# Moving GpSimd's work in a kernel's input stage to VectorE, and one reduction ahead of three tiles

## The chip, the cores and the metric

One core of a Trainium2 chip runs the whole program in one launch. The engines of a core work at the same time, each through a queue of its own in order: TensorE (PE in the profile; its weight loads are PEld), VectorE (DVE), ScalarE (ACT), GpSimd (POOL) and SyncE (SP), which here issues nearly all DMAs. They wait for each other through semaphores. The metric is the device time of one execution in microseconds (us), less is better.

## What is computed

Two layers over 1024 tokens of width 1024, in float32. The first is latent attention: an input projection gives 384 q latents, 256 kv latents, 64 shared rotary key columns and 1024 gate columns; the latents are normalised and projected to 8 heads. The second is a gated convolution module (31 taps). Cut to the part that the change touches:

```python
h = rmsnorm(x, mla_norm_g)
z = h @ w_in                                   # 1024 x 1728
q_lat, kv_lat, k_pe, gate = split(z, [384, 640, 704])
q  = rmsnorm(q_lat, q_norm_g) @ w_qb           # 8 heads of 128 + 64 rotary
kv = rmsnorm(kv_lat, kv_norm_g) @ w_kvb
q_pe, k_pe = apply_rope(q_pe), apply_rope(k_pe)
x = x + (attention(q, k, v) * silu(gate)) @ w_out
# then the convolution layer, x + ..., and a last rmsnorm
```

## The kernel before, in words

Activations lie transposed, 128 channels by 1024 tokens to a tile. Each matrix product is made of three passes over rounded numbers: every operand is split into a high half (rounded) and a low half (what the rounding left), and a product is high x high, high x low, low x high (`mm3`, lines 136 to 139: L137, L138 and L139 in the profile). So each weight tile that arrives needs a copy on ScalarE (`wh_...`, L104) and a subtraction (`wl_...`, L106), and the third matmul of a tile is the first that reads the low half. In `load_w` the subtraction is GpSimd's unless the caller names an engine; in `split_early`, which splits weights of the second layer early and stores their low halves (`sl_cg`, L120) in DRAM for later, it is GpSimd's too.

The input stage, the first 196 us, runs so:

- Three accumulators (`acc3`: kv latents and rotary key) are built while x arrives, and VectorE adds up the squares of x (`ssum`).
- Then come eleven tiles `in_tile(n)`, named b0 to b10, of 48 matmuls each: b0 to b2 are the q latents, b3 to b10 the gates of the eight heads. Between b8 and b9 stand four tiles for the rotary part of q (`ps_qr`, 18 matmuls each).
- For the scale of a norm, squares are added up tile by tile (`lat_evac`, L302: `zskv`, `zsq_`), then `col_sums32` folds the 1024 sums of a row: a transposition on VectorE (L158), a reduction on VectorE (L160, `part...`), and one small matmul (L162, `cskv`, `csq`), after which small instructions give the scale, which goes out to DRAM and comes back spread over all partitions (`spread_dma`: `rowq`, then `Fq`). `lat_norm` does that for the kv latents after b1 and for the q latents after b5.
- VectorE also computes the angles of the rotary tables meanwhile (`trig_...`, about 25 instructions for each half of the tokens, L369 to L385), and multiplies each gate tile out of PSUM (`gt`, L340).

PSUM has six accumulator buffers in this stage, so a tile of matmuls needs the one of three tiles earlier to have been emptied. Weight tiles rotate through five buffers (`w`), raw weights through two (`wraw`).

TensorE's order is the program's (a manual schedule). The order of the other engines is worked out when the kernel is built, by a scheduler with a model of its own; it stands fixed in the program. After the input stage GpSimd scales the softmax rows, adds products in the convolution, and scales outputs at the end.

Of the kernel before, what the change touches and what calls it, by code (L numbers as in the profile page):

```python
# [18 lines left out]
P = 128  # L19
# [45 lines left out]
def hybrid_body(ctx, tc, xT, xP, pos, cols, w1a, w1b, wqr, wqk, wv, wo, wc, we, out):  # L65
# [15 lines left out]
    ones = const.tile([P, P], F32, name="ones")  # L81
    g.memset(ones, 1.0)

# [4 lines left out]
    warm = const.tile([P, 1], F32, name="warm")  # L88
    s.activation(warm, ones[:, 0:1], AF.Copy)
    small = ctx.enter_context(tc.tile_pool(name="small", bufs=1))  # L90
# [5 lines left out]

    def load_w(src, n, nm, alloc=None, eng=g):
        if alloc is None:
            def alloc(name):
                return wp.tile([P, 1024], F32R, tag="w", bufs=5, name=name)  # L100
        raw = wp.tile([P, 1024], F32, tag="wraw", name=f"wr_{nm}")
        sp.dma_start(raw[:, :n], src)
        hi = alloc(f"wh_{nm}")
        s.activation(hi[:, :n], raw[:, :n], AF.Copy)  # L104
        lo = alloc(f"wl_{nm}")
        eng.tensor_tensor(lo[:, :n], raw[:, :n], hi[:, :n].bitcast(F32), ALU.subtract)  # L106
        return hi, lo
# [4 lines left out]
    def split_early(src, nm):  # L112
        raw = wp.tile([P, 1024], F32, tag="wraw", name=f"sr_{nm}")
        sp.dma_start(raw, src)
        hi = wp.tile([P, 1024], F32R, tag="w", bufs=5, name=f"sh_{nm}")
        lo = wp.tile([P, 1024], F32R, tag="w", bufs=5, name=f"sl_{nm}")
        for a in range(2):
            cs = sl(a, CH)
            s.activation(hi[:, cs], raw[:, cs], AF.Copy)
            g.tensor_tensor(lo[:, cs], raw[:, cs], hi[:, cs].bitcast(F32), ALU.subtract)  # L120
        loS[nm] = tc.dram_tile([P, 1024], F32, name=f"loS{nm}")
        sp.dma_start(loS[nm], lo.bitcast(F32))
# [30 lines left out]

    def col_sums32(src, ntok, tile_, alloc, nm):

        n = ntok // 32
        tr = tile_.rearrange("p (j f) -> p j f", f=32)
        v.transpose(tr, src.rearrange("p (r j) -> p j r", r=32))  # L158
        part = small.tile([P, 32], F32, tag="part", bufs=1, name=f"part{nm}")[:, :n]
        reduced[nm] = v.tensor_reduce(part, tr, AX.X, ALU.add)  # L160
        ps = alloc(f"cs{nm}")[:, :n]
        pe.matmul(ps, mod32, part, start=True, stop=True)  # L162
        return ps
# [96 lines left out]
    for k in range(KD):  # L260
        xs[k] = ar.tile([P, T], F32, tag="zg", bufs=5, name=f"xs{k}")
        if k == 0 or k % 2 == 1:
            first, many = k, 1 if k in (0, KD - 1) else 2
            pair = load_w(w1a[:, 384 * k : 384 * (k + many)], 384 * many, f"a{k}", eng=v)
        wh, wl = (w_[:, 384 * (k - first) : 384 * (k - first + 1)] for w_ in pair)
        for c in range(2):
            sp.dma_start(xs[k][:, sl(c, CH)], xT[sl(k), sl(c, CH)])
        if k == 0:
# [13 lines left out]

    def lat_norm(zg, zs, n, gname, dh, dl, nm):
        F = tmp(f"F{nm}")
        Fc = inv_sqrt(col_sums32(zs, T, F, pstat, nm), 1.0 / (n * P), 1e-6, nm, extra=Rc)
        Fr = small.tile([P, 32], F32, tag="Fr", bufs=1, name=f"Fr{nm}")
        v.tensor_tensor(Fr, Fc, Rc, ALU.mult)
        spread_dma(Fr, T, F, nm)
        for i in range(n):
            v.scalar_tensor_tensor(zg[i], zg[i], cc(gname, i), F, ALU.mult, ALU.mult)  # L290
            s.activation(dh[i], zg[i], AF.Copy)
            v.tensor_tensor(dl[i], zg[i], dh[i].bitcast(F32), ALU.subtract)

    def lat_evac(ps, zg, zs, i, nm):
        for c in range(2):
            s.activation(zg[i][:, sl(c, CH)], ps[c], AF.Copy)
        if i == 0:
            s.activation(zs, zg[i], AF.Square)
        else:
            sq = tmp(f"zsq{nm}{i}")  # L300
            s.activation(sq, zg[i], AF.Square)
            g.tensor_tensor(zs, sq, zs, ALU.add)  # L302

    def in_tile(n):
        wh, wl = load_w(w1b[n], 1024, f"b{n}")
        ps = []
# [25 lines left out]
    ps_q1 = in_tile(1)  # L332
    lat_norm(zgkv, zskv, NKV, "gkv", kvh, kvl, "kv")
    ps_q2 = in_tile(2)
# [11 lines left out]
    for i, ps in enumerate((ps_q0, ps_q1, ps_q2)):  # L346
        lat_evac(ps, zgq, zsq_, i, "q")
    for h in range(3):
        gate_tile(h)
        split_early(wc[16 + h], f"cg{h}")  # L350
    lat_norm(zgq, zsq_, NQL, "gq", qnh, qnl, "q")


# [45 lines left out]
    def rope_pair(pr):  # L399
# [13 lines left out]
        for j in range(2):  # L413
            t1, t2 = tmp(f"rt1{pr}{j}"), tmp(f"rt2{pr}{j}")
            v.tensor_tensor(t1, A if j == 0 else B, cosT, ALU.mult)
            g.tensor_tensor(t2, B if j == 0 else A, sinT, ALU.mult)
            v.tensor_tensor(t1, t1, t2, ALU.subtract if j == 0 else ALU.add)
# [12 lines left out]
    gate_tile(7)  # L430

    es_pe.close()
    es_ap.close()
# [538 lines left out]
    def e_out(part):  # L972
# [9 lines left out]
        for m in range(KD):  # L982
# [6 lines left out]
            if c == 0:  # L989
                sp.dma_start(out[sl(m), cols_], x_)  # L990
            elif m % 2:
                sp.dma_start(out[sl(m // 2, 2 * P), cols_].rearrange("(a p) n -> p a n", a=2),
                             x1p[m // 2][:, :, n0:n1])
# [112 lines left out]
```

## Time and profile before

| | |
|---|---|
| three runs | 919.27, 922.48, 923.67 us (median 922.48) |
| the profiled execution | 922.44 us |
| its span, first to last instruction | 920.7 us |
| busy: PE, PEld, DVE, ACT, POOL | 897.9, 746.5, 648.8, 504.6, 440.6 us |
| mean granted clock of TensorE | 0.990 of full speed |
| input stage, to the last gate matmul | about 0 to 192 us of the span |

Of the page, part 1 gives the busy time of each engine; part 2 cuts the span into 40 slices and shows, under PEclk, the clock that TensorE was granted. The view of waits lists for each engine whom it waited for and how long. The view of windows gives busy times and the granted clock of chosen stretches. The timeline has one line for each instruction, or for several equal ones in a row (`x3`), with its start, its duration, and in brackets how long its engine had been idle and what ended that.

### The profile page before, as it was taken

Reading aid. Unit: us, or ns where it says so; the run is one execution under the profiler, and the core shown is the slowest. Engines: PE = TensorE matmul, PEld = TensorE weight load, DVE = VectorE, ACT = ScalarE, POOL = GpSimd, SP = SyncE. Lnnn points to the kernel's source line nnn. Section 1 sums busy time; section 2 is a strip of 40 time slices with the busy share of each in tenths; the row PEclk is TensorE's granted clock in tenths of the full one; section 3 lists DMA queues with packets and bytes.
Section 4 is the critical chain, followed back from the end, with each engine's and each line's share of the span. In section 5 each row is a group of like instructions: output and inputs, shape, how many; then the busy total and the mean of one; then the engine's idle time right before and its main releaser. Section 6 shows DMA issues by size and latency. Waiting matters only on the chain.

```text
span 920.7 us, 12418 instructions
## 1 busy us (share of the span) xinstructions
PE 897.9 (98%) x4432; PEld 746.5 (81%) x4432; DVE 648.8 (70%) x1073; ACT 504.6 (55%) x839; POOL 440.6 (48%) x370
## 2 busy tenths in 40 slices
PE   9999799999999999999999999999999999999996
PEld 7888588788898888978887887888888887778996
DVE  7478943756566656667454858999999998697543
ACT  8535244346465545565343446766666774677732
POOL 0333442725263332443234449999999993000034
PEclk9999989999999999999999999999999999999998
DMA  7214453485062232352183421111112322245714
GB/s 265 91 70 126 153 198 141 145 281 154 22 203 84 62 125 84 126 194 92 43 294 92 159 82 47 46 47 46 46 47 69 94 101 99 73 137 175 271 65 138
DMA packets 39662, 110.19 MB, mean 120 GB/s; under 512 B 5232, under 2 KB 8304, under 8 KB 39600
## 3 DMA queue, kind: packets, MB, share of 16 engines
q1 hardware_dynamic: 39520, 109.14, 35.6%
q8 instruction: 35, 0.57, 0.3%
q14 instruction: 27, 0.22, 0.1%
q0 software_dynamic: 80, 0.26, 0.1%
HBM read 83.93 MB, written 24.92 MB: 118 GB/s over the span
## 4 chain that ended last, share of the span: by engine, by line
PE 84%; DVE 7%; DMA 3%; ACT 2%; POOL 1%; issue 1%; SPq 0%; DVEq 0%; ACTq 0%; POOLq 0%
PE e L137 3%; PE e L139 3%; PE cb L138 3%; PE e L138 3%; PE cb L139 3%; PE cb L137 3%; PE cg L137 3%; PE cg L138 3%; PE cg L139 3%; PE T L545 3%; PE ca L137 3%; PE ca L139 3%; PE ca L138 3%; PE o L139 3%; PE o L137 3%; PE o L138 3%
## 5 line engine op out<-in xcount | busy, mean ns | idle before, releaser
L797 POOL TENSOR_TENSOR dcv<-dcv,pkb 128x512 f32<-128x512 f32 (+1 forms) x126 | 157.9, 1256 | 8.6 <-ACT pkb L796 1.0
L796 ACT ACTIVATE pkb<-u,taps 128x512 f32<-128x512 f32 (+1 forms) x126 | 83.8, 675 | 55.6 <-POOL dcv L797 50.8
L532 POOL TENSOR_SCALAR P<-P,st 128x128 f32<-128x128 f32 (+3 forms) x64 | 48.4, 757 | 122.5 <-DVE st L531 115.4
L808 DVE SCALAR_TENSOR_TENSOR av<-u,taps,av 128x512 f32<-128x512 f32 (+1 forms) x135 | 91.7, 687 | 1.2 <-ACT av L802 1.1
L810 DVE SCALAR_TENSOR_TENSOR cv<-su,gsum,cv 128x512 f32<-128x512 f32 (+1 forms) x117 | 80.6, 689 | 0.4
L987 POOL TENSOR_TENSOR x<-x,rbe 128x512 f32<-128x512 f32 (+1 forms) x16 | 16.2, 1051 | 127.0 <-DMA rbe<-rowe 127.0
L554 ACT ACTIVATE pth<-T 128x512 fp32r<-128x512 f32 (+1 forms) x96 | 46.1, 490 | 51.2 <-PE T L545 44.0
L555 DVE TENSOR_TENSOR ptl<-T,pth 128x512 fp32r<-128x512 f32 (+1 forms) x96 | 52.3, 554 | 30.4 <-ACT pth L554 30.0
L139 PE MATMUL ps_b<-xgh,wl_b 128*128 128x512 f32 x176 | 70.7, 402 | 1.2 <-POOL wl_b L106 1.2
L137 PE MATMUL ps_b<-xgh,wh_b 128*128 128x512 f32 x176 | 70.8, 403 | 0.0
L138 PE MATMUL ps_b<-xgl,wh_b 128*128 128x512 f32 x176 | 70.5, 401 | 0.0
L106 POOL TENSOR_TENSOR wl_o<-wr_o,wh_o 128x1024 fp32r<-128x1024 f32 x16 | 39.4, 2465 | 59.2 <-PE o L139 30.3
L137 PE MATMUL e<-a_y,wh_e 128*128 128x256 f32 (+1 forms) x192 | 61.7, 322 | 0.0
L139 PE MATMUL e<-a_y,wl_e 128*128 128x256 f32 (+1 forms) x192 | 61.5, 320 | 0.0
L138 PE MATMUL e<-a_y,wh_e 128*128 128x256 f32 (+1 forms) x192 | 61.4, 320 | 0.0
L529 ACT ACTIVATE P<-S,st 128x128 f32<-128x128 f32 (+3 forms) x64 | 47.5, 742 | 23.9 <-DVE st L527 18.7
L106 POOL TENSOR_TENSOR wl_b<-wr_b,wh_b 128x1024 fp32r<-128x1024 f32 x11 | 31.0, 2817 | 53.9 <-PE acc L138 36.7
L137 PE MATMUL cg<-a_h,wh_cg 128*128 128x512 f32 x128 | 51.7, 404 | 0.0
L138 PE MATMUL cb<-a_h,wh_cb 128*128 128x512 f32 x128 | 50.8, 397 | 0.8 <-DVE a_h L727 0.8
L139 PE MATMUL o<-a_og,wl_o 128*128 128x512 f32 x128 | 51.0, 398 | 0.3 <-POOL wl_o L106 0.3
L137 PE MATMUL o<-a_og,wh_o 128*128 128x512 f32 x128 | 51.0, 400 | 0.0
L137 PE MATMUL cb<-a_h,wh_cb 128*128 128x512 f32 x128 | 50.8, 397 | 0.0
(320 smaller groups left out, 2730.2 us busy)
## 6 DMA issues: line engine op xcount, KB each, us to landing
wr_o<-in_wo_dram SPq DMA_DIRECT2D x16, 512.0 KB, 4.1
wr_e<-in_we_dram SPq DMA_DIRECT2D x14, 512.0 KB, 4.6
wl_e<-loSe SPq DMA_DIRECT2D x14, 512.0 KB, 3.9
wr_b<-in_w1b_dram SPq DMA_DIRECT2D x11, 512.0 KB, 3.3
xs<-in_xT_dram SPq DMA_DIRECT2D x16, 256.0 KB, 5.6
sr_cg<-in_wc_dram SPq DMA_DIRECT2D x8, 512.0 KB, 4.5
loScg<-sl_cg SPq DMA_DIRECT2D x8, 512.0 KB, 3.8
gateS<-gt SPq DMA_DIRECT2D x8, 512.0 KB, 2.8
```

What stands on the lines that cost most here:

```text
L106: eng.tensor_tensor(lo[:, :n], raw[:, :n], hi[:, :n].bitcast(F32), ALU.subtract)
L137: pe.matmul(ps, wh, xh, start=start, stop=False)
L138: pe.matmul(ps, wh, xl, start=False, stop=False)
L139: pe.matmul(ps, wl, xh, start=False, stop=stop)
L529: s.activation(pr[:, :nk], ps[:, off : off + nk], AF.Exp, bias=st[:, 0:1], accum_out=st[:, 1:2])
L532: g.tensor_scalar(pr[:, :nk], pr[:, :nk], st[:, 2:3], 1.0, ALU.mult, ALU.mult)
L554: s.activation(hi[:, n0:], pt[:, n0:], AF.Copy)
L555: v.tensor_tensor(lo[:, n0:], pt[:, n0:], hi[:, n0:].bitcast(F32), ALU.subtract)
L796: s.activation(pk, lag(src, i), AF.Copy, scale=tap(of, i))
L797: g.tensor_tensor(acc, acc, pk, ALU.add)
L808: v.scalar_tensor_tensor(a_, lag(E, i), tap(dwe, i), a_, ALU.mult, ALU.add)
L810: v.scalar_tensor_tensor(c_, lag(su, i), tap(gsum, i), c_, ALU.mult, ALU.add)
```

## The change

- `ones` is filled by VectorE instead of GpSimd, and ScalarE's warming instruction moves behind a DMA.
- Until the end of the input stage, all subtractions for low halves (`load_w` and `split_early`) go to VectorE; a list of one element, `early_eng`, is switched to GpSimd after the last gate tile. The additions of squares in `lat_evac` and one product of each rotary pair go to VectorE as well.
- `col_sums32` is cut in two: `fold32` (transposition and reduction) and the matmul. For the q latents, `lat_fold` is now called ahead of the three gate tiles, and `lat_norm` with the matmul stays behind the third.
- The first half of the first x tile is loaded by a DMA on ScalarE's queue.
- At the end, the last part's first two output rows of tiles go out in two DMAs, the second on ScalarE's queue, instead of one.

```diff
-    g.memset(ones, 1.0)
+    v.memset(ones, 1.0)
...
-    s.activation(warm, ones[:, 0:1], AF.Copy)
...
+    early_eng = [v]
+
+    def load_w(src, n, nm, alloc=None, eng=None):
...
-        eng.tensor_tensor(lo[:, :n], raw[:, :n], hi[:, :n].bitcast(F32), ALU.subtract)
+        (eng or early_eng[0]).tensor_tensor(lo[:, :n], raw[:, :n], hi[:, :n].bitcast(F32), ALU.subtract)
...
-            g.tensor_tensor(lo[:, cs], raw[:, cs], hi[:, cs].bitcast(F32), ALU.subtract)
+            early_eng[0].tensor_tensor(lo[:, cs], raw[:, cs], hi[:, cs].bitcast(F32), ALU.subtract)
...
-    def col_sums32(src, ntok, tile_, alloc, nm):
-
+    def fold32(src, ntok, tile_, nm):
         n = ntok // 32
         tr = tile_.rearrange("p (j f) -> p j f", f=32)
         v.transpose(tr, src.rearrange("p (r j) -> p j r", r=32))
         part = small.tile([P, 32], F32, tag="part", bufs=1, name=f"part{nm}")[:, :n]
         reduced[nm] = v.tensor_reduce(part, tr, AX.X, ALU.add)
+        return part
...
         xs[k] = ar.tile([P, T], F32, tag="zg", bufs=5, name=f"xs{k}")
+        if k == 0:
+            s.dma_start(xs[k][:, :CH], xT[sl(k), :CH])
+            s.activation(warm, ones[:, 0:1], AF.Copy)
...
-            sp.dma_start(xs[k][:, sl(c, CH)], xT[sl(k), sl(c, CH)])
+            if k > 0 or c > 0:
+                sp.dma_start(xs[k][:, sl(c, CH)], xT[sl(k), sl(c, CH)])
...
-            g.tensor_tensor(zs, sq, zs, ALU.add)
+            v.tensor_tensor(zs, sq, zs, ALU.add)
...
+    folded = lat_fold(zsq_, "q")
     for h in range(3):
         gate_tile(h)
         split_early(wc[16 + h], f"cg{h}")
-    lat_norm(zgq, zsq_, NQL, "gq", qnh, qnl, "q")
+        if h == 2:
+            lat_norm(zgq, folded, NQL, "gq", qnh, qnl, "q")
...
-            g.tensor_tensor(t2, B if j == 0 else A, sinT, ALU.mult)
+            v.tensor_tensor(t2, B if j == 0 else A, sinT, ALU.mult)
...
     gate_tile(7)
 
+    early_eng[0] = g
...
+            elif part == 2 and m < 2:
+                (s if m else sp).dma_start(out[sl(m), cols_], x_)
```

TensorE's order stays the same to the last row. On VectorE, before, this stands around the q latents' fold (`Fq`, `partq`); `trig_..1` are the angles of the second half of the tokens, `kp` and `krl` the rotary key, `gt0` to `gt2` the gates of tiles b3 to b5:

```order
L385 TENSOR_SCALAR trig_ang1_950<-trig_nn1_951 128x512
L340 TENSOR_TENSOR gt1_802<-ps_b40_752,R_499 128x512
L394 SCALAR_TENSOR_TENSOR kp2_979<-kp2_979,col_61,sinT_920 128x1024
L393 TENSOR_TENSOR kp_440<-kp_440,cosT_919 128x1024
L395 TENSOR_TENSOR kp_440<-kp_440,kp2_979 128x1024
L340 TENSOR_TENSOR gt1_802<-ps_b41_777,R_499 128x512
L397 TENSOR_TENSOR krl_121<-kp_440,krh_120 128x1024
L340 TENSOR_TENSOR gt2_873<-ps_b50_823,R_499 128x512
L158 STREAM_TRANSPOSE Fq_888<-zsq__661 128x1024
L160 TENSOR_REDUCE partq_890<-Fq_888 128x32
```

The same place of VectorE's queue in the changed kernel, with the addition of squares (L318) ahead of the fold and the low half of tile b5 (`wl_b5`) behind it:

```order
L318 TENSOR_TENSOR zsq__661<-zsqq2_672,zsq__661 128x1024
L393 TENSOR_SCALAR trig_nh1_952<-trig_nh1_952 128x512
L158 STREAM_TRANSPOSE Fq_675<-zsq__661 128x1024
L356 TENSOR_TENSOR gt0_735<-ps_b30_685,R_499 128x512
L121 TENSOR_TENSOR sl_cg1_814<-sr_cg1_811,sh_cg1_813 128x512 x2
L356 TENSOR_TENSOR gt0_735<-ps_b31_710,R_499 128x512
L394 TENSOR_TENSOR trig_nn1_951<-trig_nn1_951,trig_nh1_952 128x512
L397 SCALAR_TENSOR_TENSOR trig_ang1_950<-trig_nh1_952,trig_ang1_950 128x512
L160 TENSOR_REDUCE partq_677<-Fq_675 128x32
L107 TENSOR_TENSOR wl_b5_825<-wr_b5_821,wh_b5_823 128x1024
```

The fold has moved from behind the angles, the rotary key and the gates of b4 to a place ahead of most of them; it now shares the queue with low halves that GpSimd made before. On the way from the q latents' scale to the rotary tiles, VectorE's queue in the changed kernel has these rows (`Frq` is the scale, `zgq` the scaled latents, `qnl` their low halves, `sl_cg4`, `sl_cg5` and `wl_b8` work that was GpSimd's):

```order
L121 TENSOR_TENSOR sl_cg4_1124<-sr_cg4_1121,sh_cg4_1123 128x512 x2
L356 TENSOR_TENSOR gt3_1045<-ps_b61_1020,R_499 128x512
L187 SCALAR_TENSOR_TENSOR rtq_895<-sqq_896,rtq_895 128x32
L107 TENSOR_TENSOR wl_b8_1135<-wr_b8_1131,wh_b8_1133 128x1024
L303 TENSOR_TENSOR Frq_905<-rtq_895,rtR_506 128x32
L356 TENSOR_TENSOR gt4_1116<-ps_b70_1066,R_499 128x512
L306 SCALAR_TENSOR_TENSOR zgq0_658<-zgq0_658,col_61,Fq_675 128x1024
L306 SCALAR_TENSOR_TENSOR zgq1_659<-zgq1_659,col_61,Fq_675 128x1024
L306 SCALAR_TENSOR_TENSOR zgq2_660<-zgq2_660,col_61,Fq_675 128x1024
L121 TENSOR_TENSOR sl_cg5_1195<-sr_cg5_1192,sh_cg5_1194 128x512 x2
L356 TENSOR_TENSOR gt4_1116<-ps_b71_1091,R_499 128x512
L308 TENSOR_TENSOR qnl0_124<-zgq0_658,qnh0_121 128x1024
```

Before, `Frq` stood right behind the other small instructions of the scale; now the second halves of tile b6's work (`gt3` from its second accumulator, which ends with b6) and `wl_b8` stand ahead of it.

## Rows read from the trace of the kernel before

**Rows 1.** The page, part 1: busy us, share of the span, instructions.

```profile
PE 897.9 (98%) x4432; PEld 746.5 (81%) x4432; DVE 648.8 (70%) x1073; ACT 504.6 (55%) x839; POOL 440.6 (48%) x370
```

**Rows 2.** Waits of PE: total us, times, longest us.

```profile
PE csq L162 <- DVE partq L160: 6.8, 1, 6.8
...
PE ps_b L139 <- POOL wl_b L106: 1.2, 1, 1.2
...
PE acc L137 <- ACT xgh L272: 0.7, 1, 0.7
```

**Rows 3.** Windows: us, each engine's busy time (x instructions), granted clock, DMA.

```profile
52.00:108.00 56.00, 56.00 (x242) 44.88 (x241) 50.09 (x70) 22.62 (x31) 22.11 (x11) 1.00 0.36 118
...
108.00:115.00 7.00, 0.34 (x2) 0.00 (x0) 6.26 (x5) 3.13 (x4) 5.57 (x3) 0.69 0.54 198
115.00:121.00 6.00, 5.81 (x15) 4.67 (x16) 1.30 (x5) 4.10 (x5) 3.77 (x3) 0.51 0.37 130
...
166.00:171.00 5.00, 3.82 (x17) 2.79 (x16) 5.00 (x2) 2.10 (x4) 5.00 (x3) 1.00 0.21 84
```

**Rows 4.** Timeline of PE, tiles b5/b6, first rotary tile, tile b9.

```profile
107.95 0.40 PE L139 MATMUL ps_b<-xgh,wl_b 128*128 128x512 f32 x1
115.19 0.64 PE L162 MATMUL csq<-partq,mod 128*128 128x32 f32 x2 [6.84 <-DVE partq L160]
...
120.89 0.39 PE L137 MATMUL ps_b<-xgh,wh_b 128*128 128x512 f32 x1
...
151.68 0.39 PE L137 MATMUL ps_qr<-qnh,wh_qr 128*128 128x512 f32 x1
...
168.77 0.40 PE L138 MATMUL ps_b<-xgl,wh_b 128*128 128x512 f32 x1
170.35 0.50 PE L139 MATMUL ps_b<-xgh,wl_b 128*128 128x512 f32 x1 [1.18 <-POOL wl_b L106]
```

**Rows 5.** Groups of VectorE, 20 to 196 us: busy us, mean ns, idle before.

```profile
L379 DVE SCALAR_TENSOR_TENSOR trig_ang<-trig_nn,trig_ang 128x512 f32<-128x512 f32 x8 | 10.6, 1327 | 0.1
...
L379 DVE SCALAR_TENSOR_TENSOR trig_ang<-trig_nh,trig_ang 128x512 f32<-128x512 f32 x8 | 10.2, 1273 | 0.1
...
L158 DVE STREAM_TRANSPOSE Fq<-zsq__661 128x1024 f32<-128x1024 f32 x1 | 1.9, 1921 | 0.0
...
L383 DVE SCALAR_TENSOR_TENSOR trig_ang<-trig_nn,trig_ang 128x512 f32<-128x512 f32 x2 | 1.4, 694 | 0.0
...
L393 DVE TENSOR_TENSOR kp<-kp,cosT 128x1024 f32<-128x1024 f32 x1 | 1.2, 1222 | 0.0
...
L106 DVE TENSOR_TENSOR wl_a<-wr_a,wh_a 128x384 fp32r<-128x384 f32 x1 | 0.6, 554 | 0.0
```

**Rows 6.** Timelines of POOL and of VectorE, 63 to 67 us.

```profile
63.20 2.88 POOL L106 TENSOR_TENSOR wl_b<-wr_b,wh_b 128x1024 fp32r<-128x1024 f32 x1 [9.02 <-PE ps_b L139]
...
63.85 2.78 DVE L379 SCALAR_TENSOR_TENSOR trig_ang<-trig_nh,trig_ang 128x512 f32<-128x512 f32 x1
```

**Rows 7.** Timeline of ACT: the last squares of the q latents.

```profile
87.05 1.06 ACT L301 ACTIVATE zsqq<-zgq 128x1024 f32<-128x1024 f32 x1
```

**Rows 8.** Timelines of SP and VectorE: the q latents' scale out and back.

```profile
122.90 0.32 SPq L195 DMA_DIRECT2D rowq<-Frq  x1
...
130.88 6.66 DVE L290 SCALAR_TENSOR_TENSOR zgq<-zgq,col,Fq 128x1024 f32<-128x1024 f32 x3 [6.30 <-DMA Fq<-rowq]
```

**Rows 9.** Start: timeline of SP (two x halves), chain of waits (second weights).

```profile
1.66 0.91 SPq L267 DMA_DIRECT2D xs<-in_xT_dram  x2
...
3.08 5.49 DMA wr_a<-in_w1a_dram
```

**Rows 10.** End: timeline of VectorE, the last outputs.

```profile
914.55 2.08 DVE L985 TENSOR_TENSOR x<-x,bce 128x256 f32<-128x256 f32 x6 [1.78 <-ACT rb L981]
```

**Rows 11.** Chain of waits (split weights); timeline of POOL (b6's low half).

```profile
101.16 5.87 DMA sr_cg<-in_wc_dram
...
110.43 3.22 POOL L106 TENSOR_TENSOR wl_b<-wr_b,wh_b 128x1024 fp32r<-128x1024 f32 x1
```

More of the change, by code (lines that the diff above doesn't have):

```diff
@@ L95, in hybrid_body @@
     ogS = [[tc.dram_tile([P, CH], F32, name=f"ogS{h}{c}") for c in range(2)] for h in range(NH)]
-    def load_w(src, n, nm, alloc=None, eng=g):
+    early_eng = [v]
+    def load_w(src, n, nm, alloc=None, eng=None):
         if alloc is None:
@@ L160, in col_sums32 @@
         reduced[nm] = v.tensor_reduce(part, tr, AX.X, ALU.add)
+        return part
+    def col_sums32(src, ntok, tile_, alloc, nm):
+        n = ntok // 32
+        part = fold32(src, ntok, tile_, nm)
         ps = alloc(f"cs{nm}")[:, :n]
@@ L281, in hybrid_body, with lat_fold, lat_norm @@
     square_x(KD - 1)
-    def lat_norm(zg, zs, n, gname, dh, dl, nm):
+    def lat_fold(zs, nm):
         F = tmp(f"F{nm}")
-        Fc = inv_sqrt(col_sums32(zs, T, F, pstat, nm), 1.0 / (n * P), 1e-6, nm, extra=Rc)
+        return F, fold32(zs, T, F, nm)
+    def lat_norm(zg, folded, n, gname, dh, dl, nm):
+        F, part = folded
+        ps = pstat(f"cs{nm}")[:, :32]
+        pe.matmul(ps, mod32, part, start=True, stop=True)
+        Fc = inv_sqrt(ps, 1.0 / (n * P), 1e-6, nm, extra=Rc)
         Fr = small.tile([P, 32], F32, tag="Fr", bufs=1, name=f"Fr{nm}")
@@ L301, in lat_evac @@
             s.activation(sq, zg[i], AF.Square)
-            g.tensor_tensor(zs, sq, zs, ALU.add)
+            v.tensor_tensor(zs, sq, zs, ALU.add)
     def in_tile(n):
-        wh, wl = load_w(w1b[n], 1024, f"b{n}")
+        wh, wl = load_w(w1b[n], 1024, f"b{n}", eng=v)
         ps = []
@@ L332, in hybrid_body @@
     ps_q1 = in_tile(1)
-    lat_norm(zgkv, zskv, NKV, "gkv", kvh, kvl, "kv")
+    lat_norm(zgkv, lat_fold(zskv, "kv"), NKV, "gkv", kvh, kvl, "kv")
     ps_q2 = in_tile(2)
```

## The prediction

> **What bounds the kernel.** The page first: TensorE is busy for 898 of 921 us [rows 1], so the time is its matmuls, at the cadence they have, plus the places where it stands still. A tile of 48 matmuls follows another without a break (56 us hold 242 records, 0.23 us each [rows 3]; 11.2 us a tile). Next, PE's list of waits: one is large, 6.8 us, for VectorE's `partq`; GpSimd's low half of a tile costs 1.2, the start 0.7 [rows 2]. Then the stage of the large one. In the timeline the last matmul of tile b5 starts at 107.95, `csq` at 115.19 [rows 4]: 7.24 us against a cadence of 0.23, so 7.0 are lost. The windows show more: the granted clock is 0.69 of full in 108 to 115 and 0.51, that is 1.2 instead of 2.4 GHz, in 115 to 121, where 15 matmuls are recorded [rows 3]. From `csq` to the first matmul at the old cadence, 115.19 to 120.89 [rows 4], twelve large matmuls and the small pair run: 5.7 us, which at 0.23 each and some 0.25 for the pair would be 3.05. So the idle time costs another 2.65 us afterwards. Last, who holds `partq` up: VectorE works for 50 of the 56 us before [rows 3], and it does so on instructions that are stretched. One `trig_ang` step takes 2.78 us beside GpSimd's 2.88 [rows 6]; the sixteen of one kind average 1.33 and 1.27 where the two of the same shape at L383 take 0.69 [rows 5].
>
> **What it removes.** With the fold ahead of the gates, `csq` finds its sums ready: 7.0 + 2.65 = 9.65 us. The check, forward from the squares: ScalarE ends them at 88.1 [rows 7]. Behind that VectorE adds them (1.22), transposes (1.92), and before the reduction (1.22, as any of that size) passes two halves of `gt0`, two of `sl_cg1` and two steps of the angles, six at about 0.69, and a small one of 0.4 [rows 5]: 88.1 + 1.22 + 1.92 + 0.4 + 4.1 + 1.22 = 97.0. TensorE asks at 108. Eleven us of cover; if VectorE came 11 us later the wait would be back.
>
> The second wait is at b9: its matmul over the low half starts 1.58 us after its neighbour instead of 0.23, so 1.35 [rows 4], because GpSimd makes that low half behind two rotary products. In VectorE's queue it stands behind three rotary products and an addition, 4 x 1.22, and takes 1.22 [rows 5]: 6.1 us after the second rotary tile has been copied out. The two remaining rotary tiles are 2 x 18 x 0.23 = 8.3 us of matmuls, and the copy some 0.7, and the low half is wanted 0.5 later: 8.8 against 6.8, so it is there 2.0 us early. I count the 1.35 as gone.
>
> **What it adds.** Thirty-five instructions on VectorE: eleven low halves and seven sums and products of 1024 columns at 1.22, twelve of 512 at about 0.69, four of 384 at 0.55, one small [rows 5]: 22.0 + 8.3 + 2.2 = 32.5 us. What it gives back is the stretching, of which the angles alone have 8 x (1.33 - 0.69) + 8 x (1.27 - 0.69) = 9.7 us [rows 5]. In the crowded 56 us before `csq`, five low halves, two sums and three pairs of halves come in, 6.1 + 2.4 + 4.1 = 12.6, and the fold of 3.1 moves in: 50.1 + 12.6 + 3.1 - 9.7 = 56.1 of 56 us. So VectorE fits, barely, and only if the stretching goes. As its order has the urgent rows ahead of the angles, I ask what is late next at two places:
>
> - The low half of b5 stands right behind the reduction: 97.0 + 1.22 = 98.2. b5 starts at 107.95 + 0.23 - 11.2 = 97.0 and wants it two matmuls later, 97.5. That is 0.7 late with the squares where they are; but the kv scale ahead of them is reached without the stretched steps (two of 2.1 us extra against two added of 1.22), which brings the squares some 1.5 us forward. Between 0.7 us of wait and none.
> - The rotary tiles. Before, the first starts at 151.68 [rows 4]; without 9.65 and the start's gain below it is 141.6, and it wants its own low half at 142.1. The q latents' scale `Frq` now stands behind `gt3` and `wl_b8`, which wait for the end of b6. That end is 11.2 after `csq` at 108, 119.4: plus two halves, a gate, a low half and small ones, 1.4 + 0.7 + 1.22 + 0.2, `Frq` is at 122.9, just when it went out before [rows 8]. On SP it has a gate's store ahead of it now, some 0.8 later. Out, back and into `zgq` took 7.98 us [rows 8]: 131.7. Three scalings 3.7, three halves 2.1, three low halves 3.7, and 0.55: 141.8. A margin of 0.3 us where there were 10.
>
> For both together I take 0.5 us, out of 0 to 4 (upper end: the larger of the DMA trips 2 us longer, and 2 us at the two tiles together).
>
> **Start and end.** The second weights land 5.49 us after SP issues them at 3.08 [rows 9], and ScalarE and VectorE follow from that, so the start moves only as far as they do. One of two x DMAs in front, 0.46 us of SP's time (0.91 for two) [rows 9], is gone: 0.4. At most it is the 0.7 us that PE waits for the first x [rows 2]; below nothing, to -0.5, if the issue on ScalarE's queue, of the same 0.46, delays its first copies. The Trainium skill ("DMA: Bandwidth & Descriptors", Issuing engines are not separate DMA queues) says that initiating on several engines saves only the sequencer's time for issuing; by that rule it is 0.46 and never 0.7, and the sum differs by 0.3. At the end, VectorE's last product is done at 914.55 + 2.08 = 916.63 [rows 10] and the last DMA hangs on it; the pair that is split is the first, so the last DMA stays where it was. I count 0, with 0.3 either way. `ones` on VectorE lies ahead of anything that waits.
>
> **Sum.** 7.0 + 2.65 + 1.35 + 0.4 - 0.5 = 10.9 us. The profiled execution took 922.44 (span 920.7, 1.7 around it), 0.04 off the median of the three, so it stands for them: 922.4 - 10.9 = **911.5 us**. After the input stage the other engines' order is the same and TensorE is busy to the end, so nothing takes the gain back there.
>
> **Rivals.**
> *The next weights are late instead (918.7).* Before, GpSimd makes b6's low half from 110.43 to 113.65, behind split weights whose DMA lands at 107.03 [rows 11]. If that chain kept its times, b6 would wait from 108.65 to 113.65 and the clock would fall again: 5.0 + 2.65 of the 11.4 gone, 3.75 left. For it: the DMA is 5.87 us long and the order of what follows is kept. Against it: the chain starts from the gate `gt0`, which the stretched angles hold up; in the new order the split weights are asked for ahead of that gate's store, and VectorE makes two halves and a low half in 2.6 us where GpSimd takes 3.2 for the low half alone.
>
> *Both thin margins break (917).* Two waits of 1.5 us and one fall of the clock: 3 + 2.65 less 0.5 already counted, 922.4 - 10.9 + 5.2 = 916.7. For it: margins of 0.3 and -0.7 us. Against: the clock stayed at 1.00 through the 1.58 us at b9 [rows 3].
> *VectorE becomes the bound (929, slower).* If the long instructions are not GpSimd's doing, nothing is given back. Then it has 65.8 us of work in the 56, is 9.8 late at b6, and the clock falls at b5 and at b6, 5.3; the three scalings of the q latents stay at 6.66 us [rows 8] instead of 3.7, which with the margin of 0.3 is 2.6 at the rotary tiles: 17.7 against 11.4, so 922.4 + 6.3 = 928.7. It decides from 3.5 us of backlog on, that is if VectorE gets back less than 6.3 of the 9.7 us. For it: the 56.1 us of work in 56 leave no room. Against it: the long ones stand beside GpSimd's rows [rows 6].
>
> **Chances.** The sum 0.70 (its own range 908 to 915), both margins 0.16, the next weights 0.09, VectorE 0.05. What a measurement can tell from no change is 0.5%, 4.6 us: faster means below 917.9. The first two are, the third falls just inside, the fourth is called slower: faster 0.86, same 0.09, slower 0.05. Range 907.5 to 917.5: it leaves out the last two rivals and a little below, where the start gains 0.7 and no margin breaks.
>
> **What would show it.** In the new profile: no wait of PE at `csq`, and 1.00 in PEclk around 108; `trig_ang` at 0.69 throughout; no wait at b9; waits of under 1 us at b5 and at the first rotary tile, or none; VectorE nearly full from 80 to 105. It is wrong if PE waits over 2 us for a `wl_b`, `wl_qr` or `qnl`, or if `trig_ang` stays long without GpSimd.

## The result and the profile after

Changed kernel: 907.53 to 909.12 us in four runs, median 908.37; the kernel before beside it 921.26 (four runs). The ratio is 0.9859, with a 95% interval of 0.983 to 0.9887: 13.0 us less. A second set of runs of the same changed kernel gave 0.9884 (0.9869 to 0.9899), 10.7 us less. The forecast was 911.5, 10.9 less. The profiled execution took 909.12 us (span 907.2) against 922.44 (span 920.7), 13.3 less.

The page of the changed kernel, part 1, answers to [rows 1]:

```profile
PE 894.3 (99%) x4432; PEld 745.0 (82%) x4432; DVE 650.4 (72%) x1108; ACT 504.4 (56%) x839; POOL 370.6 (41%) x335
```

VectorE has 35 instructions more, 32.5 us by the durations of before, and is busy only 1.6 us longer: some 31 us of stretching have gone over the whole kernel, where the prediction counted 9.7 for the angles alone.

PE's waits in the changed kernel, beside [rows 2]:

```profile
PE S L541 <- DMA rq<-ropeS: 0.2, 1, 0.2
```

`csq`, the `ps_b` of b9 and the first `acc` are off the list. What is left are waits of the attention and of the end. The line shown is new: the first product that reads the rotary part of q waits for its load.

Windows of the changed kernel at the places of [rows 3], shifted by the time gained:

```profile
52.00:107.00 55.00, 55.00 (x238) 44.37 (x237) 47.57 (x81) 23.66 (x32) 0.00 (x0) 1.00 0.47 158
107.00:114.00 7.00, 7.00 (x32) 5.68 (x32) 6.83 (x10) 3.47 (x5) 0.00 (x0) 1.00 0.50 149
114.00:120.00 6.00, 6.00 (x27) 4.82 (x26) 2.54 (x7) 4.38 (x6) 0.00 (x0) 1.00 0.46 180
```

TensorE is full in every one and its clock is 1.00, where it was 0.69 and 0.51 behind the stall. VectorE works 47.6 of the 55 us ahead of `csq`: there is room.

PE's timeline at the first reader of b5's low half, at `csq`, at the first rotary tile and at b9, beside [rows 4]:

```profile
96.31 0.40 PE L140 MATMUL ps_b<-xgh,wl_b 128*128 128x512 f32 x1
...
107.05 0.30 PE L300 MATMUL csq<-partq,mod 128*128 128x32 f32 x2
...
140.88 0.39 PE L138 MATMUL ps_qr<-qnh,wh_qr 128*128 128x512 f32 x1
...
141.34 0.40 PE L140 MATMUL ps_qr<-qnh,wl_qr 128*128 128x512 f32 x1
...
158.22 0.40 PE L140 MATMUL ps_b<-xgh,wl_b 128*128 128x512 f32 x1
```

The distance to before grows along these milestones: 1.01 us at the first matmul of b0 (40.41 to 39.40), 8.14 at `csq` (115.19 to 107.05), 10.80 at the first rotary tile (151.68 to 140.88), 12.23 where the input stage ends (192.38 to 180.15), 12.74 at the last matmul of `e` (909.64 to 896.90), 13.5 at the end of the span. So: start 1.01, wait 7.13, clock 2.66, b9 1.43, and 1.3 us behind the input stage.

Groups of VectorE from 20 to 185 us, beside [rows 5], and then its timeline around the fold:

```profile
L397 DVE SCALAR_TENSOR_TENSOR trig_ang<-trig_nn,trig_ang 128x512 f32<-128x512 f32 x8 | 5.5, 688 | 0.1
L397 DVE SCALAR_TENSOR_TENSOR trig_ang<-trig_nh,trig_ang 128x512 f32<-128x512 f32 x8 | 5.5, 687 | 0.1
```

```profile
92.41 1.21 DVE L160 TENSOR_REDUCE partq<-Fq 128x32 f32<-128x1024 f32 x1
93.54 1.22 DVE L107 TENSOR_TENSOR wl_b<-wr_b,wh_b 128x1024 fp32r<-128x1024 f32 x1
...
131.22 3.68 DVE L306 SCALAR_TENSOR_TENSOR zgq<-zgq,col,Fq 128x1024 f32<-128x1024 f32 x3 [6.25 <-DMA Fq<-rowq]
...
140.02 0.55 DVE L107 TENSOR_TENSOR wl_qr<-wr_qr,wh_qr 128x384 fp32r<-128x384 f32 x1
...
154.69 1.22 DVE L107 TENSOR_TENSOR wl_b<-wr_b,wh_b 128x1024 fp32r<-128x1024 f32 x1
```

The angles take 0.69 us throughout. `partq` is done at 93.6, 13.4 us ahead. The low half of b5 is done at 94.8, its first reader starts at 96.31; that of the first rotary tile at 140.57, against 141.34; that of b9 at 155.9, against 158.22. The three scalings take 3.68 us where they took 6.66 [rows 8].

ScalarE's timeline, with the first x half [rows 9], the copy of the second weights (`wh_a`) and the last squares [rows 7]; then the same copy in the kernel before:

```profile
0.74 0.42 ACTq L269 DMA_DIRECT2D xs<-in_xT_dram  x1
...
7.58 0.85 ACT L105 ACTIVATE wh_a<-wr_a 128x768 fp32r<-128x768 f32 x1 [0.33 <-DMA wr_a<-in_w1a_dram]
...
84.28 1.06 ACT L317 ACTIVATE zsqq<-zgq 128x1024 f32<-128x1024 f32 x1
```

```profile
8.60 0.85 ACT L104 ACTIVATE wh_a<-wr_a 128x768 fp32r<-128x768 f32 x1 [0.99 <-DMA wr_a<-in_w1a_dram]
```

The x half goes out 0.92 us sooner than on SP, where it went out at 1.66; the copy of the second weights starts 1.02 sooner; and the squares end at 85.3, 2.8 sooner.

### The profile page after: what moved, and what is told of

It is laid out like the page before. It is cut to its first block, busy times and chain, and to the rows that moved or that the text cites. A ratio compares the mean times of both kernels' runs of the same rounds, so it can differ in the third digit from the quotient of the medians.

```text
span 907.2 us, 12407 instructions
## 1 busy us (share of the span) xinstructions
PE 894.3 (99%) x4432; PEld 745.0 (82%) x4432; DVE 650.4 (72%) x1108; ACT 504.4 (56%) x839; POOL 370.6 (41%) x335
## 4 chain that ended last, share of the span: by engine, by line
PE 90%; DMA 3%; DVE 2%; ACT 2%; POOL 1%; issue 1%; SPq 1%; DVEq 0%; ACTq 0%; POOLq 0%
PE ps_b L138 5%; PE ps_b L140 5%; PE ps_b L139 5%; PE cb L139 3%; PE cb L140 3%; PE cb L138 3%; PE cg L138 3%; PE cg L139 3%; PE cg L140 3%; PE e L138 3%; PE e L140 3%; PE e L139 3%; PE T L564 3%; PE ca L138 3%; PE ca L140 3%; PE ca L139 3%
## 5 line engine op out<-in xcount | busy, mean ns | idle before, releaser
L107 POOL TENSOR_TENSOR wl_qk<-wr_qk,wh_qk 128x640 fp32r<-128x640 f32 x8 | 12.6, 1571 | 174.3 <-PE ps_b L139 167.7
L107 POOL TENSOR_TENSOR wl_o<-wr_o,wh_o 128x1024 fp32r<-128x1024 f32 x16 | 41.5, 2596 | 55.4 <-PE o L140 21.8
L139 PE MATMUL cb<-a_h,wh_cb 128*128 128x512 f32 x128 | 50.8, 397 | 0.8 <-DVE a_h L746 0.8
L138 PE MATMUL ca<-a_h,wh_ca 128*128 128x512 f32 x128 | 50.8, 397 | 0.0
```

The lines of the kernel that those rows point to most:

```text
L107: (eng or early_eng[0]).tensor_tensor(lo[:, :n], raw[:, :n], hi[:, :n].bitcast(F32), ALU.subtract)
L138: pe.matmul(ps, wh, xh, start=start, stop=False)
L139: pe.matmul(ps, wh, xl, start=False, stop=False)
```

## The experiments

Two theories at the outset. A: GpSimd's instructions stretch VectorE's and hold up the weights behind them, so that their going is what removes the wait at `csq`. B: the late place of the fold alone made that wait. Ratios are to the kernel before in the same set of runs, with the 95% interval.

**The fold alone**, from the kernel before (`e1_fold_alone`).

```diff
+    folded = lat_fold(zsq_, "q")
     for h in range(3):
         gate_tile(h)
         split_early(wc[16 + h], f"cg{h}")
-    lat_norm(zgq, zsq_, NQL, "gq", qnh, qnl, "q")
+        if h == 2:
+            lat_norm(zgq, folded, NQL, "gq", qnh, qnl, "q")
```

> The kernel before with the fold of the q latents ahead of the gates and nothing else; GpSimd keeps its low halves, sums and products. Theory A (GpSimd's instructions stretch VectorE's, and the weights behind them are late too): no wait at `csq`, but the wait passes on to b6, whose low half GpSimd makes from about 110.4 to 113.7: PE waits 4 to 5 us there, at b6's first or third matmul, the clock falls to 0.5 again, the wait of 1.2 us at b9 stays; `trig_ang` stays at a mean of about 1.3 us. Gain 2 to 4 us, some 918.5 to 920.5. Theory B (the late place of the fold alone made the wait): no wait over 1 us at b6, clock 1.00, a gain of 7.0 + 2.65 = 9.65 us, about 912.8.

Measured: 917.89 us, 0.9958 (0.9943 to 0.9973). Its timeline of PE at the place:

```profile
108.02 0.30 PE L295 MATMUL csq<-partq,mod 128*128 128x32 f32 x2
109.68 0.50 PE L137 MATMUL ps_b<-xgh,wh_b 128*128 128x512 f32 x1 [1.36 <-ACT wh_b L104]
...
112.78 0.80 PE L139 MATMUL ps_b<-xgh,wl_b 128*128 128x512 f32 x1 [2.36 <-POOL wl_b L106]
```

`csq` no longer waits, and b6's weights do, twice. They are late in a row of three engines, as ScalarE's and GpSimd's timelines tell:

```profile
106.92 0.63 ACT L399 ACTIVATE trig_nh<-trig_ang 128x512 f32<-128x512 f32 x1 [4.99 <-DVE trig_ang L398]
...
108.59 1.04 ACT L104 ACTIVATE wh_b<-wr_b 128x1024 fp32r<-128x1024 f32 x1
```

```profile
109.76 2.97 POOL L106 TENSOR_TENSOR wl_b<-wr_b,wh_b 128x1024 fp32r<-128x1024 f32 x1 [5.54 <-ACT wh_b L104]
```

ScalarE idles 5 us for VectorE's angles before it can copy b6's weights, and GpSimd then takes 3 us. The wait at `csq` had lain over this one. The rival of the prediction, the next weights late, is this case; 918.7 was worked out for it.

**The engines alone** (`e2_engines_alone`): the changed kernel with the fold called behind the gates, and with the start and the end of before.

> The changed kernel with the fold called behind the gates again, as before, and with the start and the end of before; only the move of GpSimd's work to VectorE is left. Theory A: `trig_ang` at 0.69 us throughout, `partq` done before PE asks, though by less than 2 us; no wait over 0.5 us at `csq`, clock 1.00, no wait at b9: a gain of 7.0 + 2.65 + 1.35 = 11.0 us, about 911.4. Theory B: the fold still stands behind 12.6 us of added work, `csq` waits 3 us or more and the clock falls: a gain of 1.35 + at most 4, about 917 to 921.

Measured: 910.73 us, 0.9884 (0.9869 to 0.9899), and no entry for `csq` among the waits. VectorE's timeline:

```profile
104.18 2.08 DVE L159 STREAM_TRANSPOSE Fq<-zsq__661 128x1024 f32<-128x1024 f32 x1
...
106.48 1.22 DVE L161 TENSOR_REDUCE partq<-Fq 128x32 f32<-128x1024 f32 x1
107.79 1.29 DVE L407 SCALAR_TENSOR_TENSOR kp<-kp,col,sinT 128x1024 f32<-128x1024 f32 x1
```

`partq` ends at 107.70 and `csq` starts at 107.75, 0.24 late. That looks like a win for stretching alone, but one thing more has moved: the fold stands ahead of the rotary key (`kp`, `krl`), though nobody called it earlier. The scheduler put it there. Before, the rotary key and two gates lay ahead of it. So this run doesn't tell the two causes apart; the next does.

**The engines moved and the fold held at its old place** (`e9_fold_last`), from the kernel with the engines alone.

```diff
-    lat_norm(zgq, lat_fold(zsq_, "q"), NQL, "gq", qnh, qnl, "q")
...
     v.tensor_tensor(krl, kp, krh.bitcast(F32), ALU.subtract)
+    v.scalar_tensor_tensor(zsq_[:, :1], krl[:, :1].bitcast(F32), 0.0, zsq_[:, :1], ALU.mult, ALU.add)
+    lat_norm(zgq, lat_fold(zsq_, "q"), NQL, "gq", qnh, qnl, "q")
```

> The kernel with the engines alone moved, but the fold of the q latents held at its old place in VectorE's queue, behind the rotary key's last row `krl` (a row of one column that adds zero times `krl` to the sums holds it there). With the engines alone the fold had also moved ahead of the rotary key: of `kp`, `krl` and the gates that stood before it. Theory A' (the place in VectorE's queue decides; what the stretching gives back the added work takes): `partq` comes 5 to 10 us after PE asks at 107.5, `csq` waits that long, the clock falls to 0.5, and of the 11 us only b9's 1.35 and at most 2 us are left: 917 to 921. Theory A (the stretching decides): a wait of 2 us at most, 911 to 914.

Measured: 923.74 us, 1.0017 (1.0001 to 1.0032): the whole gain is gone, where Theory A' had left 1.35 us of it and at most 2 more. The waits of PE, VectorE's timeline and its groups:

```profile
PE csq L297 <- DVE partq L161: 9.9, 1, 9.9
```

```profile
115.36 1.92 DVE L159 STREAM_TRANSPOSE Fq<-zsq__661 128x1024 f32<-128x1024 f32 x1
```

```profile
L391 DVE SCALAR_TENSOR_TENSOR trig_ang<-trig_nn,trig_ang 128x512 f32<-128x512 f32 x8 | 5.5, 690 | 0.2
```

The angles are short and the wait is longer than ever: VectorE starts the fold at 115.36, before at 111.96, and PE waits 9.9 us where it was 6.8 [rows 2]. Theory A falls as the cause of the wait. The place in VectorE's queue makes it: with the early place and stretched angles there was no wait at `csq` (fold alone), with the late place and short angles it is 9.9 us. The stretching that goes pays for the work that comes.

**The changed kernel with the fold called behind the gates** (`e5_fold_behind`), and **the changed kernel again** (`e6_after_again`), in one set of runs.

```diff
-    folded = lat_fold(zsq_, "q")
...
-        if h == 2:
-            lat_norm(zgq, folded, NQL, "gq", qnh, qnl, "q")
+    lat_norm(zgq, lat_fold(zsq_, "q"), NQL, "gq", qnh, qnl, "q")
```

> The changed kernel with nothing but the fold of the q latents called behind the three gate tiles again, as before; start, end and engines stay changed. Theory A (GpSimd's instructions gone is what removes the wait; the fold's place only buys slack): `partq` ends within 1 us of the moment at which PE asks, as with the engines alone (107.70 against 107.75), so a wait of 0 to 0.8 us at `csq`, clock 1.00: 0 to 0.8 us above the changed kernel, some 908.4 to 909.2. Theory B (the fold's place matters too): 3 us or more of wait, 911 or more.

> The changed kernel as it is, for the runs beside it and for the scatter of one profiled execution. 908.4, a ratio of 0.986. If the half microsecond that the attention gained between the two profiled executions, and the 0.4 us at the last four matmuls, are scatter, they come out otherwise here (from the first `pj` to the last `e`: 717.26 us before, 716.75 after, 716.1 to 716.5 in the four other kernels); if the change makes them, 716.75 and 0.43 us again.

Measured: 910.0 us, 0.9877 (0.9863 to 0.989), against 909.75, 0.9884 (0.9869 to 0.9899). The moved call is worth nothing that can be measured. It buys slack, 13.4 us against none, on a place the scheduler had already mended. From the first `pj` to the last `e` the changed kernel took 716.84 us this time (716.75, and 717.26 before): the eleven kernels that don't wait over 0.5 us for `rq` lie between 716.0 and 717.5, so the half microsecond there is scatter.

**GpSimd kept busy beside VectorE** (`e4_gpsimd_beside`): twelve additions that nobody reads; all other engines have the same order row for row.

```diff
     folded = lat_fold(zsq_, "q")
+    beside = ar.tile([P, CH], F32, name="beside")
+    for i in range(12):
+        g.tensor_tensor(beside, (zgq[2] if i == 0 else xgh[i % 8].bitcast(F32))[:, :CH],
+                        xgl[i % 8].bitcast(F32)[:, CH:], ALU.add)
```

> The changed kernel with twelve additions of 512 columns on GpSimd into a tile that nobody reads, from the moment the last q latent is copied out (about 84); the order of every other engine is the same row for row. Theory A: each of the twelve takes 1.3 to 1.9 us beside VectorE, VectorE's instructions between 85 and 105 are held up by most of that time, `partq` and the low half of b5 behind it come 5 to 11 us later, PE waits 4 to 9 us at b5's third matmul and the clock falls to 0.5: 6 to 12 us slower than the changed kernel, 914 to 920. If the long instructions are not GpSimd's doing: `trig_ang` stays at 0.69, nothing waits, 908.4.

Measured: 916.26 us, 0.9942 (0.9926 to 0.9959), 5.3 to 7.6 us slower than the changed kernel by its two ratios; the input stage ends at 187.1 instead of 180.2, 7.0 later. GpSimd's timeline, then VectorE's:

```profile
84.19 1.30 POOL L367 TENSOR_TENSOR beside<-zgq,xgl 128x512 f32<-128x512 f32 x1 [82.88 <-ACT zgq L312]
85.58 19.01 POOL L367 TENSOR_TENSOR beside<-xgh,xgl 128x512 f32<-128x512 f32 x11
```

```profile
87.91 1.53 DVE L397 TENSOR_SCALAR trig_nh<-trig_nh 128x512 f32<-128x512 f32 x1
89.36 2.09 DVE L158 STREAM_TRANSPOSE Fq<-zsq__661 128x1024 f32<-128x1024 f32 x1
91.38 0.64 DVE L356 TENSOR_TENSOR gt<-ps_b,R 128x512 f32<-128x512 f32 x1
...
96.00 1.75 DVE L401 SCALAR_TENSOR_TENSOR trig_ang<-trig_nh,trig_ang 128x512 f32<-128x512 f32 x1
97.66 1.21 DVE L160 TENSOR_REDUCE partq<-Fq 128x32 f32<-128x1024 f32 x1
98.79 1.21 DVE L107 TENSOR_TENSOR wl_b<-wr_b,wh_b 128x1024 fp32r<-128x1024 f32 x1
```

The stretching is GpSimd's doing: 0.69 becomes up to 1.79 and 0.42 becomes 1.53, with no other edit. The low half of b5 comes at 100.0 instead of 94.8, and PE waits 4.0 us for it, then 1.3 at the rotary tile:

```profile
PE ps_b L140 <- DVE wl_b L107: 4.0, 1, 4.0
```

Not all rows suffer: the transposition (2.09), the reduction (1.21) and the product out of PSUM (0.64) keep the durations they have in the changed kernel (2.07, 1.21, 0.65). The low half of b5 keeps its 1.21 too, although other low halves (`sl_cg`) go from 0.68 to as much as 1.80 beside GpSimd: it begins 0.15 us ahead of an addition of GpSimd's, and there the addition is the long one, 2.22 us where one alone took 1.30:

```profile
98.94 2.22 POOL L367 TENSOR_TENSOR beside<-xgh,xgl 128x512 f32<-128x512 f32 x1
```

The Trainium skill ("SBUF — State Buffer", Who interferes with whom) says that the two engines hold one pair of ports in turn, the later one blocked until the other's instruction ends; that row agrees, and so does the size of the losses: none here exceeds one of GpSimd's rows (at most 1.1 us beside additions of 1.3 to 2.2, and 2.09 of 2.88 in [rows 6]).

**The early split weights back on GpSimd** (`e8_split_back`).

```diff
-            early_eng[0].tensor_tensor(lo[:, cs], raw[:, cs], hi[:, cs].bitcast(F32), ALU.subtract)
+            g.tensor_tensor(lo[:, cs], raw[:, cs], hi[:, cs].bitcast(F32), ALU.subtract)
```

> The changed kernel with the early split weights' low halves (`sl_cg`, twelve of 512 columns) on GpSimd again: work that nobody waits for in this stage. Theory A: GpSimd holds VectorE up by most of what the twelve take there (1.3 to 1.7 us each), more than the 0.69 each that VectorE is relieved of; the angles beside them go above 0.8 us on the mean, and the low half of b5 or of a later tile comes late by 0.5 to 1.5 us: 909 to 911. Rival (load counts, not company): VectorE has 8.3 us less to do, nothing waits, 908.4 or a little less.

Measured: 908.99 us, 0.9871 (0.9857 to 0.9886), no wait in the input stage: my expectation missed, and the rival's held as far as the waits go. VectorE's groups, then its busy time in the first 180 us, in the changed kernel run again and in this one:

```profile
L397 DVE SCALAR_TENSOR_TENSOR trig_ang<-trig_nh,trig_ang 128x512 f32<-128x512 f32 x8 | 7.1, 888 | 0.1
L397 DVE SCALAR_TENSOR_TENSOR trig_ang<-trig_nn,trig_ang 128x512 f32<-128x512 f32 x8 | 6.5, 810 | 0.1
```

```profile
0.00:180.00 180.00, 129.50 (x180) 1.00 0.49 168
```

```profile
0.00:180.00 180.00, 128.98 (x168) 1.00 0.48 168
```

The move takes 8.2 us of rows off VectorE. The company costs the angles 2.6 us (8 x 0.20 and 8 x 0.12) and other rows, `zsq`, `krl`, `qnl` and a conversion, 3.8 more, so VectorE's busy time, in which rows that overlap count once, falls by 0.5 us alone. Here the company costs most of what it takes off; in the run above, which took nothing off, all of it was cost.

**The rotary products back on GpSimd** (`e7_rope_back`), and the same with **the last gate's store on ScalarE's queue** (`e11_rope_gate_store`); that store in the changed kernel is `e10_gate_store`.

```diff
-            v.tensor_tensor(t2, B if j == 0 else A, sinT, ALU.mult)
+            g.tensor_tensor(t2, B if j == 0 else A, sinT, ALU.mult)
```

```diff
-        sp.dma_start(gateS[h], gt)
+        (s if h == 7 else sp).dma_start(gateS[h], gt)
```

> The changed kernel with the rotary products `t2` on GpSimd again; the low halves stay on VectorE. Theory A (stretching): the four products take 2.4 to 3.1 us on GpSimd, VectorE's rotary products and `wl_b9` beside them are stretched, and of the 2.3 us by which `wl_b9` is early in the changed kernel nothing is left: a wait of 0.5 to 1.5 us at b9, up to the 1.35 that went away; 908.9 to 909.9. Rival (b9 waited because its low half stood in GpSimd's queue): no wait at b9, 908.4.

> The changed kernel with one DMA moved: the last gate's store goes out on ScalarE's queue, behind the activation that makes it, instead of on SP's, where the loads of the rotary parts (`rq`) stand behind it from 173.7 to 182.1. If that queue holds the loads, they go out some 8 us earlier and the wait at the first `S` that reads `rq` (0.17 and 0.48 us in the two executions of the changed kernel) is gone: 0.2 to 0.5 us less, 908 to 909, which only the trace can tell. If the loads wait for the stores of the rotary parts themselves, nothing changes.

> The kernel with the rotary products `t2` back on GpSimd, which waited 2.7 us at the first `S` for `rq`, with the last gate's store on ScalarE's queue as well. If SP's queue, held by that store, made the loads late: the wait is gone and with it the clock's fall behind it, some 3 us less than 912.8, about 909.5. If the rotary rows themselves are late (the last is stored at 178.3 instead of 174.0): 1 to 2.7 us of wait stay, 911 to 912.8.

Measured: the rotary products back, 912.82 us, 0.9907 (0.9893 to 0.9921). b9 does not wait, although three of VectorE's rotary rows are stretched from 1.22 to 3.4 us, but only just. Its low half, which was 2.3 us early, is done at 158.09, and its first reader starts at 158.15 (VectorE's timeline, then PE's):

```profile
156.88 1.21 DVE L107 TENSOR_TENSOR wl_b<-wr_b,wh_b 128x1024 fp32r<-128x1024 f32 x1
```

```profile
158.15 0.49 PE L140 MATMUL ps_b<-xgh,wl_b 128*128 128x512 f32 x1
```

The rival had it right that there is no wait with the low half out of GpSimd's queue, Theory A that the stretching takes the whole margin. The loss is at a place that no theory had named, the attention's first rotary product (chain of waits, then the window from 178 to 182 us):

```profile
185.49 6.68 DMA rq<-ropeS
```

```profile
178.00:182.00 4.00, 4.00 (x19) 3.22 (x18) 1.20 (x2) 1.03 (x3) 1.68 (x3) 1.00 0.99 333
```

The same window of the changed kernel, run again:

```profile
178.00:182.00 4.00, 4.00 (x19) 3.23 (x18) 0.69 (x1) 1.78 (x2) 1.74 (x3) 1.00 0.00 0
```

With the rotary rows 4.3 us later (the last is stored at 177.9, in the changed kernel at 173.6), weights and a gate's store crowd into the 4 us in which the DMA engines had been idle; their busy share is 0.99 instead of 0.00, and a load of 128 KB, the one that PE waits 2.7 us for, takes 6.7 us (4.62 and 4.98 in the chains of the changed kernel's two profiles). That the crowding makes it late fits these rows and was not tested by itself. The last gate's store is not it: with it out of the way the loads still go out from 182.4 on in the changed kernel and from 182.6, 0.6 sooner, in the rotary version, whose wait is 2.0 instead of 2.7 us, and the times are 911.96, 0.9906 (0.9887 to 0.9924), and for the changed kernel 908.73, 0.9868 (0.985 to 0.9885), with no wait at `rq` in the one execution profiled. Right ahead of the loads in SP's queue stands one of split weights (`sr_cg`), which goes out at 181.96 and 182.19; SP's longest wait there, in the changed kernel with the store moved, is this one:

```profile
SPq L115 <- POOL mask L467: 7.6, 1, 7.6
```

What would release that load sooner was not tried.

**The fold and the low halves of the tiles** on VectorE, the rest as before (`e12_fold_and_low`), from the fold alone.

```diff
-        wh, wl = load_w(w1b[n], 1024, f"b{n}")
+        wh, wl = load_w(w1b[n], 1024, f"b{n}", eng=v)
```

> The kernel before with the fold ahead of the gates and the low halves of the tiles b0 to b10 on VectorE; GpSimd keeps the early split weights, the sums of squares and the rotary products. If GpSimd's own queue made the low half of b6 late in the kernel with the fold alone, and its company costs VectorE little: no wait at b6, none at b9, about 921 - 9.65 - 1.35, that is 910 to 911. If the company decides: VectorE has 13.4 us of low halves more and is still stretched (`trig_ang` over 1.1 us on the mean), low halves come late at b5 or b8 by 1 to 3.5 us: 912 to 917.

Measured: 919.77 us, 0.9984 (0.9969 to 1.0). The waits of PE, and VectorE at the largest of them (2.8 us, b8):

```profile
PE ps_b L139 <- DVE wl_b L106: 4.6, 3, 2.8
PE S L535 <- DMA rq<-ropeS: 1.8, 1, 1.8
```

```profile
131.61 3.68 DVE L301 SCALAR_TENSOR_TENSOR zgq<-zgq,col,Fq 128x1024 f32<-128x1024 f32 x3 [6.08 <-DMA Fq<-rowq]
135.21 1.22 DVE L106 TENSOR_TENSOR wl_b<-wr_b,wh_b 128x1024 fp32r<-128x1024 f32 x1
```

Neither theory had the cause of b8's wait: its low half stands in VectorE's queue behind three scalings that wait 6 us for a DMA. In the changed kernel it stands ahead of the scale (the third order piece above). A part of the move, in an order of its own, is worth almost nothing.

**The start and the end alone**, from the kernel before (`e3_ends_alone`): the edits of the change at `ones`, `warm`, the first x half and the last outputs.

> The kernel before with the start and the end of the change alone (first x half on ScalarE's queue, ones on VectorE, two output DMAs for the last part's first pair). Start: if only SP's time for issuing is saved, tile b0's first matmul moves from 40.41 by 0.46 us to 39.95; if the first x half's earlier arrival counts in full, as the changed kernel's 39.40 suggests, by 1.0 us. End, from the last matmul of `e` to the end of the span: 11.06 us before; 10.3 if the split or the other queue shortens it (10.30 in the changed kernel), 11.1 if the 0.8 us there came from something else, as the clock at the last four matmuls. The wait of 6.8 us at `csq` stays. Total 922.4 - 1.0 - 0 to 0.8, that is 920.6 to 921.9.

Measured: 919.15 us, 0.998 (0.9971 to 0.999), 1.8 us less (0.9 to 2.7). b0 starts at 38.97. One execution scatters here: the nine kernels with the changed start have 38.97 to 39.82, on the mean 39.41, the five with the old one 39.87 to 40.82, on the mean 40.39. The start is worth 0.97 us, and it goes with the second weights: in all fourteen kernels b0 starts 31.8 to 32.3 us after ScalarE begins their copy, which is at 7.43 on the mean of the nine and at 8.41 on that of the five. The end, from the last `e` to the end of the span, is 10.42; it goes with the last four matmuls, `bce`, which take either 0.4 or 0.8 us from first to last, in kernels of both kinds. Where it is 0.4, the end takes 10.3 to 10.6 us in the six with split outputs, 10.5 and 10.6 in the two without; the split gains 0.1 at most, less than the scatter among the six.

## Why the prediction was right, and where it was not

- **7.0 at `csq` and 2.65 for the clock: right in size (7.13, 2.66), wrong in what earns them.** The size is that of the stall and of the clock behind it, whichever edit takes them away, so it does not bear out the reason. The step was "With the fold ahead of the gates, `csq` finds its sums ready". It does; but that edit alone keeps some 4 us of it (ratio 0.9958), since b6's weights are late behind it (fold alone), and without that edit the gain is the same (fold behind the gates). What earned it is the engines' move: it brought b6's weights forward and led the scheduler to put the fold ahead of the rotary key. That the place in the queue is what counts, the held fold shows.
- **"VectorE fits, barely, and only if the stretching goes": half right.** The sum of 56.1 us in 56 was too high; the window holds 47.6 in 55. It kept in the window three rows of the rotary key (L394, L393, L395 before, 3.7 us) and a low half (1.2) that the new order has behind `csq`, and it took the angles' 9.7 us for all of the stretching, where the window loses some 3 more. The stretching decides what VectorE can take on (the additions on GpSimd made the stage 7 us longer), not whether `csq` waits.
- **New waits 0.5: none.** b5's low half is 1.5 us early, not 0.7 late. The squares came 2.8 us sooner where the step took 1.5: the start's 1.0, which it left out, and the rest from rows no longer stretched. The rotary tile's margin is 0.8, forecast 0.3.
- **b9 1.35: right (1.43), for the reason given.** Its low half was 2.3 us early, forecast 2.0, and with the rotary products back on GpSimd 0.06 of that is left.
- **Start 0.4: mis-sized, 0.97.** The path was right: the start moves as far as the second weights do. But the step held their trip of 5.49 us fixed and counted the issue alone. SP issues them 0.48 us sooner, at 2.60 instead of 3.08; from the issue to the start of ScalarE's copy it is 4.8 us on the mean of the nine kernels with the changed start and 5.3 in the five others. What shortens that is open. The bound of 0.7, PE's wait for the first x, was no bound, since that wait is not on this path. The Trainium skill's rule ("DMA: Bandwidth & Descriptors", Issuing engines are not separate DMA queues), that another engine saves only time for issuing, accounts for the 0.48 and not for the rest.
- **End 0: right for the split (0.1 at most).** The other 0.4 to 0.5 us of the profiled pair is the clock at the last four matmuls, and 0.5 in the attention is scatter; neither is the change's.

The terms as measured, 7.13 + 2.66 + 1.43 + 0.97 + 0.1, make 12.3 us where the forecast had 10.9; most of the difference is the start (0.57 more) and the new waits (0.5 that did not come). The two sets of runs gave 13.0 and 10.7. The rival of the next weights was real and lay in the half of the change that was run alone. No version tried is measurably faster than the changed kernel: the three that come near it (fold behind, split weights back, gate store moved) lie at 0.9868 to 0.9877, between its own two ratios.

## What to carry to other kernels

A wait that ends last can lie over another that would have ended nearly as late: before an edit is credited with the whole of it, look up when the next thing that the waiting engine needs is ready. When a change moves work to another engine and a scheduler orders it, compare where the late instruction stands in its queue before and after, for that move may be the cause. And price company on shared engines by what it takes off as well as by what it stretches.

## What the hardware showed that was not expected

- GpSimd's company stretches some of VectorE's rows and spares others: 0.69 to as much as 1.79 and 0.42 to 1.53 us for steps of the angles, 0.68 to as much as 1.80 for low halves, nothing for the transposition, the reduction and products out of PSUM. A low half that began ahead of GpSimd's addition kept its time. GpSimd pays too: its eleven additions of 512 columns took 1.3 to 2.2 us, the one that stood alone 1.30.
- Eight loads of 128 KB took 4.7 to 6.6 us from issue to landing (median 5.8) in the changed kernel run again, where the DMA engines were idle from 178 to 182 us and the first load went out at 182.4, and 6.7 to 9.7 us (median 7.8) with the rotary products back on GpSimd, where they were 0.99 busy in the same 4 us and the first went out at 183.2.
- The last four matmuls, behind idle time, took either 0.71 or some 1.23 us in two executions of the very same program, the changed kernel. The short form goes with a higher granted clock: the windows of the changed kernel run again, then of its first profile (0.61 and 0.79, means over a stretch that 1.00 goes before and, in the first of them, 0.50 follows):

```profile
899.00:902.00 3.00, 1.23 (x4) 0.93 (x4) 0.90 (x5) 0.57 (x2) 0.20 (x1) 0.61 0.33 110
```

```profile
899.00:902.00 3.00, 0.71 (x4) 0.52 (x4) 1.36 (x8) 0.59 (x2) 0.65 (x1) 0.79 0.28 94
```
